# First products two k-tiles at a time behind half jobs of modulation, and the norm parameters and last norm ahead of the loop of rounds

## The chip, the cores and the metric

The kernel runs on one core of a Trainium2 chip. The core has a matrix engine (TensorE; PE for its matmuls, PEld for its weight loads), three engines for elementwise work (VectorE or DVE, ScalarE or ACT, GpSimd or POOL), and SyncE (SP), which issues most of the transfers between the memory of the chip and the core. Each engine works through its own list of instructions in order and waits on semaphores for the others. The metric is the device time of one execution in microseconds (us); lower is better.

## What is computed

Two blocks, each of two layers, on x of 256 tokens by 1024 columns, all in float32.

```python
# block 1, per layer
mod = silu(c) @ w_ada + b_ada                      # 6 * 1024 values: shifts, scales, gains
sh1, sc1, g1, sh2, sc2, g2 = split(mod, 6)
h = rmsnorm(x, norm1_w) * (1 + sc1) + sh1          # "modulation"
u = h @ w_in                                       # pool, conv, q, k, v and gates
x = x + g1 * (merge_of_branches(u) @ w_out)
h2 = rmsnorm(x, norm2_w) * (1 + sc2) + sh2
x = x + g2 * ((silu(h2 @ w_gate) * (h2 @ w_up)) @ w_down)

# block 2
h = layer_norm(x, ln_in_g, ln_in_b)
for l in range(2):
    mix = mixer(h)                                 # three kinds of attention
    h = layer_norm(alpha * h + mix, ln1_g, ln1_b)
    ffn = grouped_moe(h)                           # 16 experts, 2 of one group per token
    h = layer_norm(alpha * h + ffn, ln2_g, ln2_b)  # the last one is the output
```

## The kernel before, in words

**Precision.** A float32 product is built from products of parts: each operand is split into a rounded part and the rest (`split`, a cast on ACT at L278 and a subtraction on DVE at L279 for weights; `hl` holds both parts of the activations), and three matmuls (L321, L322, L323 in `xs_part`) add up one product. The first of the three needs only the cast, the second the subtraction too.

**Order.** PE's list stands in the order in which the code is written. The other engines' lists are put in order by a list scheduler; `tc.issue_after` in the code adds a constraint to it. SP's list holds the weight loads in the order of the code, each into the next unit of a ring of buffers (`use_ring`, `raw`), so a load also waits until its unit is free. A load waits in addition until the load eight places before it has landed.

**The start of the program.** SP issues c, the constants `con`, x, the masks, the bias `b_ada`, the norm rows and the positions, and behind them eight loads of w_ada (`ada_first`) and six of w_in (`first_weights`), 1 MB each. PE turns x (L472), DVE copies the turned x out (L473). `norm_scale` squares the turned x on ACT (L757) and sums over the columns with 16 matmuls by ones (L758). `ada_pe` computes 512 columns of modulation per job: 64 small matmuls (L695, 32 columns of weights by 128 elements), a copy (L682), a transpose (L685), an add of the bias (L686). `modulate` then makes, per k-tile of 128 columns, u on DVE (L769), the rounded part on ACT (L770), the rest on DVE (L771). k-tiles 0 to 3 need jobs 0 and 2 (shift and scale), k-tiles 4 to 7 need jobs 1 and 3. Products run over k-tiles 0 to 3 for q, k and v in turn (j = 0, 1, 2), with jobs 1 and 3 between them, then over k-tiles 4 to 7.

**The mixture of experts** (`moe`). The token's norm is taken, ACT casts the rounded part `hn[0]` (L1500), and POOL (first half, L1502) and DVE (second half, L1569) subtract for the rest `hn[1]`. DVE works out the two experts of each token (L1506 to L1530), PE counts the slots (L1534 to L1538), DVE makes one-hot matrices (L1546), PE gathers 64 slots per expert (L1562). Then eight pairs of experts follow (`pair`): gate products, up products, activation (L1636, L1637), transposes (L1641), copy (L1643), down products, all matmuls at L1597, and the matmuls that put the pair's result back into token order (`combine`, L1656, added to the state at L1658). Those of a pair run inside the next pair; in the last pair they stand between gate and up (`pump(2)`). The statistics of the layer's last norm are taken quarter by quarter in the last pair (L802).

**The loop of rounds.** Behind the pairs each engine reads the number of rounds from memory (L1711), and a hardware loop (L1717) repeats the eight pairs for tokens that found no slot. In the profiled execution its body is not entered; every engine still crosses it with semaphores and branches. Behind the loop, `norm_params` (L810 to L817) turns the statistics into mean and scale. In layer 0 `normalise` (L826, L827) and PE's transposes (L855) then start the next mixer. In layer 1 the gains are spread over the partitions by PE (L833), applied on DVE (L1759, L1760) and, for one quarter, on ACT and POOL (L1750 to L1752), and four output transfers are issued (L1761, L1762).

Of the kernel before, what the change touches and what calls it, by code (L numbers as in the profile page):

```python
# [11 lines left out]
F32 = mybir.dt.float32  # L12
# [8 lines left out]
P = 128  # L21
# [54 lines left out]
def kernel(ctx: ExitStack, tc: tile.TileContext, A, const, out):  # L76
# [92 lines left out]
    RING_START = (17, 18, 19, 20, 21, 15, 16, 3, 4, 8, 10, 17, 18, 19, 20, 21)  # L169
# [4 lines left out]
    RING_MOE = (22, 8, 10, 11, 0, 12, 13, 9, 17, 18, 19, 20, 21, 5, 6, 7, 3, 4)  # L174
    UNIT = {8: 2560}
# [84 lines left out]
    early, held = {}, []  # L260
# [4 lines left out]
    def split(src):  # L265
# [8 lines left out]
        with ExitStack() as es:  # L274
            if held:
                for inst in held.pop():
                    es.enter_context(tc.issue_after(inst.ins))
            S.copy(h, src)  # L278
            V.tensor_sub(lo, src, h)  # L279
# [59 lines left out]
    nc.sync.dma_start(con, const[:, :CONST_KEEP])  # L339
# [22 lines left out]
    nc.sync.dma_start(xn, A["x"].rearrange("o (a p) d -> p (o a) d", p=P))  # L362
    masks = t512()[:, :CONST_W - CONST_KEEP]
    nc.sync.dma_start(masks, const[:, CONST_KEEP:])
    stage = [t512()[:, 0:P], None]
    stage_rows(nc.sync, "b_ada", rows(A["b_ada"]), 48)
    stage_rows(nc.sync, "norm1_w", rows(A["norm1_w"]), 8)
    stage_rows(nc.sync, "norm2_w", rows(A["norm2_w"]), 8)
    posi = cst.tile([P, 2, 2], I32, name="posi")
    nc.sync.dma_start(posi[:, 0, :], A["positions"].rearrange("o (a p) -> p (o a)", p=P))  # L370
    nc.sync.dma_start(posi[:, 1, :], A["positions_2"].rearrange("o (a p) -> p (o a)", p=P))
    use_ring(RING_START)

    def first_weights(k0):

        return [raw(wview(A["w_in"], 0, k0 * P, (k0 + 4) * P, 1024 + 512 * j, 1536 + 512 * j), 4, 512) for j in range(3)]

    ada_first, w_first = {}, []
# [64 lines left out]
    V.tensor_scalar_mul(cs, cact, 0.5)  # L443

# [7 lines left out]
    V.tensor_copy(causalb, mask_of("causal"))  # L452
    chunkb = cst.tile([P, P], BF16, name="chunkb")
    V.tensor_copy(chunkb, mask_of("chunk"))
    beforeb = cst.tile([P, P], BF16, name="beforeb")
    V.tensor_copy(beforeb, mask_of("before"))
# [223 lines left out]
    def ada_out(l, j, ps):  # L680
# [3 lines left out]
        def post():  # L684
            PE.transpose(ps[:, P:T], m, ident)  # L685
# [4 lines left out]
    def ada_pe(l, j, ch):  # L690
        ps = at_bank()
        for k0, r in ch:
            for k in range(k0, k0 + r.shape[1]):
                for q in range(4):
# [1096 lines left out]
```

## Time and profile before

| | |
|---|---|
| time, three runs | 1595.78, 1597.12 (median), 1597.85 us |
| the profiled execution | 1598.5 us, its span 1596.3 us |
| PE busy in the span | 1508.8 us (95%) |
| DVE, ACT, POOL busy | 977.2, 736.9, 251.3 us |
| moved by DMA | 419.71 MB, 263 GB/s over the span |

The profile is one execution, with its times counted from the start of the span. [...] A matmul's length overlaps with its successor's; the distance of starts is the pace.

### The profile page before, as it was taken

What the parts mean: (1) busy time and instruction counts of PE and PEld (TensorE: products, weight loads), DVE (VectorE), ACT (ScalarE), POOL (GpSimd) and SP (SyncE); (2) the same over time, 40 slices, a digit from 0 to 9 for tenths busy, and PEclk for the clock granted to TensorE, in tenths of its full rate; (3) what the DMA queues carried; (4) which work ended last, traced back from release to release, by engine and by line L of the source; (5) the groups of instructions that cost most, each with busy time, mean ns of one, the idle gap of its engine ahead of it and who ended that gap; (6) DMA issues with size and microseconds to landing.
All of it is one profiled execution on the core that took longest, in us unless ns stands there. A gap on an engine that the chain in (4) does not pass through costs nothing. (4 is left out here: it accounts for less than half of the span.)

```text
span 1596.3 us, 24445 instructions
## 1 busy us (share of the span) xinstructions
PE 1508.8 (95%) x9211; PEld 1091.9 (68%) x9211; DVE 977.2 (61%) x1894; ACT 736.9 (46%) x1403; POOL 251.3 (16%) x279
## 2 busy tenths in 40 slices
PE   6999899999999999999998998999998999899996
PEld 5877788888887888888887876344436877344343
DVE  4769777777787767787657667222226776423224
ACT  3466745655446674566546565121115665211122
POOL 0333640001224263100003110000000310000000
PEclk9999999999999999999999998999998999899998
DMA  9666769656864675965535457999995648899995
GB/s 349 240 210 247 253 231 324 204 188 200 314 203 156 211 263 182 321 211 178 173 103 158 150 193 281 366 407 407 407 403 203 217 141 291 310 407 407 407 407 196
DMA packets 278476, 419.71 MB, mean 263 GB/s; under 512 B 12722, under 2 KB 147748, under 8 KB 278348
## 3 DMA queue, kind: packets, MB, share of 16 engines
q1 hardware_dynamic: 273052, 398.63, 70.6%
q0 software_dynamic: 5152, 19.14, 3.5%
q8 instruction: 77, 1.26, 0.3%
q14 instruction: 51, 0.42, 0.1%
q10 hardware_dynamic: 144, 0.26, 0.0%
HBM read 416.94 MB, written 1.05 MB: 262 GB/s over the span
## 5 line engine op out<-in xcount | busy, mean ns | idle before, releaser
L279 DVE TENSOR_TENSOR split<-raw,split 128x1024 fp32r<-128x1024 f32 (+4 forms) x330 | 412.6, 1254 | 113.1 <-ACT split L278 109.9
L289 PE MATMUL mm<-hl,split 128*128 128x512 f32 x1168 | 413.4, 397 | 0.0
L278 ACT CAST split<-raw 128x1024 fp32r<-128x1024 f32 (+4 forms) x330 | 328.8, 1000 | 130.0 <-PE mm L323 68.7
L290 PE MATMUL mm<-hl,split 128*128 128x256 f32 x1168 | 328.0, 281 | 0.6 <-DVE split L279 0.6
L289 PEld LDWEIGHTS mm<-hl,split 128*128 128x128 f32 x1168 | 219.5, 188 | 49.3 <-issue 0.9
L1597 PE MATMUL mm<-raw,xg 128*64 128x512 f32 x1024 | 233.6, 603 | 1.1 <-ACT xg L1564 1.1
L290 PEld LDWEIGHTS mm<-hl,split 128*128 128x128 f32 x1168 | 221.5, 190 | 1.1 <-DVE split L279 0.9
L1597 PEld LDWEIGHTS mm<-raw,xg 128*64 128x64 f32 x1024 | 70.2, 138 | 130.9 <-issue 113.1
L289 PE MATMUL mm<-ahl,split 128*128 128x512 f32 x352 | 123.4, 394 | 0.0
L306 ACT COPY t<-mm 128x256 f32<-128x256 f32 x152 | 56.7, 373 | 143.3 <-PE mm L290 133.4
L1597 PE MATMUL mm<-raw,t 128*64 128x512 f32 (+1 forms) x576 | 114.8, 549 | 1.5 <-ACT t L1643 1.4
L321 PE MATMUL mm<-split,hl 128*128 128x512 f32 (+4 forms) x272 | 102.1, 375 | 4.3 <-ACT split L278 3.2
L290 PE MATMUL mm<-ahl,split 128*128 128x256 f32 x352 | 98.7, 281 | 0.3 <-DVE split L279 0.3
L322 PE MATMUL mm<-split,hl 128*128 128x512 f32 (+4 forms) x272 | 96.0, 353 | 0.9 <-DVE split L279 0.8
L323 PE MATMUL mm<-split,hl 128*128 128x512 f32 (+4 forms) x272 | 96.2, 354 | 0.5 <-POOL hl L1210 0.4
L306 DVE TENSOR_TENSOR t<-mm,t 128x256 f32<-128x256 f32 x140 | 59.2, 423 | 49.5 <-ACT t L306 49.2
L1597 PEld LDWEIGHTS mm<-raw,t 128*64 128x64 f32 x576 | 39.4, 137 | 67.6 <-issue 50.8
L1673 DVE SCALAR_TENSOR_TENSOR t<-mm,s,t 128x512 fp32r<-128x512 f32 (+1 forms) x36 | 24.9, 691 | 91.8 <-ACT t L1672 91.8
L289 PEld LDWEIGHTS mm<-ahl,split 128*128 128x128 f32 x352 | 65.9, 187 | 15.0 <-ACT t L1095 0.2
L1672 ACT ACTIVATE t<-mm,s 128x512 fp32r<-128x512 f32 (+1 forms) x36 | 23.1, 640 | 106.0 <-PE mm L1597 106.0
L1643 ACT COPY t<-at 128x512 f32<-128x512 f32 x16 | 9.4, 588 | 129.9 <-PE at L1641 129.9
L290 PEld LDWEIGHTS mm<-ahl,split 128*128 128x128 f32 x352 | 66.5, 189 | 0.6 <-DVE split L279 0.6
(426 smaller groups left out, 2504.8 us busy)
## 6 DMA issues: line engine op xcount, KB each, us to landing
raw<-in_exp_w_gate_dram SPq DMA_DIRECT2D x128, 512.0 KB
raw<-in_exp_w_up_dram SPq DMA_DIRECT2D x128, 512.0 KB
raw<-in_exp_w_down_dram SPq DMA_DIRECT2D x128, 512.0 KB
raw<-in_w_in_dram SPq DMA_DIRECT2D x54, 1024.0 KB
raw<-in_w_ada_dram SPq DMA_DIRECT2D x30, 1024.0 KB
raw<-in_w_gate_dram SPq DMA_DIRECT2D x22, 1024.0 KB
raw<-in_w_up_dram SPq DMA_DIRECT2D x22, 1024.0 KB
ada<-in_w_ada_dram POOLq DMA_DIRECT2D x18, 1024.0 KB, 6.6
```

What stands on the lines that cost most here:

```text
L278: S.copy(h, src)
L279: V.tensor_sub(lo, src, h)
L289: PE.matmul(ps, h[:, k], x[k0 + k], start=first and k == 0, stop=False)
L290: PE.matmul(ps[:, :T], lo[:, k], x[k0 + k][:, :T], start=False, stop=last and k == K - 1)
L306: return S.copy(b[:, :T], ps[:, T:]), V.tensor_add(dst, ps[:, :T], b[:, :T])
L321: PE.matmul(ps[i][:, :n], xh, h[:, j], start=f, stop=False)
L322: PE.matmul(ps[i][:, :n], xh, lo[:, j], start=False, stop=False)
L323: PE.matmul(ps[i][:, :n], xl, h[:, j], start=False, stop=z)
L1597: PE.matmul(ps[64 * b:64 * b + 64, :], lhs(k, b), ws[k][b], start=k == 0, stop=k == nk - 1)
L1643: S.copy(aT, pb)
L1672: S.activation(yh[:, sl], pd_[:, :w], AF.Copy, scale=gs)
L1673: V.scalar_tensor_tensor(yl[:, sl], pd_[:, :w], gs, yh[:, sl], op0=OP.mult, op1=OP.subtract)
```

## The change

**Start.** Constants, masks, bias, norm rows and positions are loaded from ACT's queue. x comes in two halves. Jobs 0 and 2 of the modulation are split into half jobs of 256 columns (`ada_first[j, h]`), and w_in's first loads hold two k-tiles each, 1 MB for q and k together and 0.5 MB for v. `first_scale` squares x as it was loaded, with its tokens on the partitions, sums on ACT, and spreads the result with two matmuls; the 16 matmuls by ones go. Products now run over k-tiles 0 and 1, then 2 and 3, then 4 to 7, with half jobs and jobs 1 and 3 between the first six. `rotary_tables` is put behind the second modulation. The casts of three masks move from DVE to POOL.

**Routing.** The subtraction of the first half of `hn[1]` moves from POOL to DVE, behind the slot positions.

**Last pair.** The matmuls of the pair before are no longer put between gate and up; they come behind up, around the transposes. The loads of the next layer (layer 0) or two of the spread gains (layer 1) are put ahead of the last pair's down products.

**Loop.** The number of rounds is read in the middle pair. `norm_params` and, in layer 1, the whole last norm with its four output transfers stand ahead of the loop, and again at the end of its body. In layer 0 `normalise` follows the loop in smaller pieces, with the first split of the next weights behind it.

```diff
-    nc.sync.dma_start(xn, A["x"].rearrange("o (a p) d -> p (o a) d", p=P))
+    for a in range(2):
+        nc.sync.dma_start(xn[:, a], A["x"][0, a * P:(a + 1) * P])
...
-        return [raw(wview(A["w_in"], 0, k0 * P, (k0 + 4) * P, 1024 + 512 * j, 1536 + 512 * j), 4, 512) for j in range(3)]
+        qk_, v_ = [raw(wview(A["w_in"], 0, k0 * P, (k0 + 2) * P, a, b), 2, b - a) for a, b in ((1024, 2048), (2048, 2560))]
+        w_first[k0] = [qk_[:, :, 0:512], qk_[:, :, 512:1024], v_]
     for h_ in range(2):
-        for j in (h_, 2 + h_):
-            ada_first[j] = k_chunks(A["w_ada"], 0, KD, 512 * j, 512 * j + 512)
-        if h_ == 0:
-            w_first.append(first_weights(0))
+        for j in (0, 2):
+            ada_first[j, h_] = k_chunks(A["w_ada"], 0, KD, 512 * j + 256 * h_, 512 * j + 256 * h_ + 256)
+        first_weights(2 * h_)
+    for j in (1, 3):
+        ada_first[j] = k_chunks(A["w_ada"], 0, KD, 512 * j, 512 * j + 512)
...
+    def first_scale():
+        ss, y, h, z, rs = small(2), small(2), small(2), small(2), small(2)
+        sq = unit(13, "sq").rearrange("p (a d) -> p a d", a=2)
+        for i in range(2):
+            S.activation(sq[:, i], xn[:, i], AF.Square, accum_out=ss[:, i:i + 1])
...
+            PE.matmul(pb[:, i * P:(i + 1) * P], rs[:, i:i + 1].to_broadcast([P, P]), ident, start=True, stop=True)
...
-            ada_pe(0, 0, ada_first[0])
-            ada_pe(0, 2, ada_first[2])
+            for j in (0, 2):
+                ada_pe(0, j, ada_first[j, 0], 0)
             pump()
-            w_first.append(first_weights(4))
-            modulate(hl, 0, 0, "norm1_w", acc, range(4))
+            first_weights(4)
+            modulate(hl, 0, 0, "norm1_w", acc, range(2))
+            for k0 in (0, 2):
+                for j in range(3):
...
+                    xs_part(pss[j], [(k0, w_first[k0][j])], hl, 512, KD, 1)
+                    if j < 2 and k0 == 0:
+                        ada_pe(0, 2 * j, ada_first[2 * j, 1], 1)
+                    elif j < 2:
+                        ada_pe(0, 1 + 2 * j, ada_first[1 + 2 * j])
+                if k0 == 0:
+                    first_weights(6)
+                    modulate(hl, 0, 0, "norm1_w", acc, range(2, 4))
+            last = modulate(hl, 0, 0, "norm1_w", acc, range(4, 8))
+            with tc.issue_after(last.ins):
+                rotary_tables()
...
-                    if q == 0:
-                        G.tensor_sub(hn[1][:, i, sl], y[:, i, sl], hn[0][:, i, sl])
...
-        for i in range(2):
-            last = V.tensor_sub(hn[1][:, i, 512:], y[:, i, 512:], hn[0][:, i, 512:])
+        with tc.issue_after(placed.ins):
+            for sl in (slice(0, 256), slice(256, 512), slice(512, 1024)):
+                for i in range(2):
+                    last = V.tensor_sub(hn[1][:, i, sl], y[:, i, sl], hn[0][:, i, sl])
...
-            if done:
-                pump(2)
             proj(pu, xs, wu, KD)
...
+                if p == NPAIR // 2:
+                    loads, (rounds,) = nc.values_load_multi_w_load_instructions(nri[0:1, 0:1], min_val=1, max_val=4)
...
-        rounds = nc.values_load(nri[0:1, 0:1], min_val=1, max_val=4)
-        if l + 1 < L:
-            mixer_first(l + 1)
+        keep = sml.tile([P, 8], F32, tag="keep", name=nm("keep"), bufs=1)
+        norm_params(keep)
+        if l + 1 == L:
+            last_norm(keep, lnb)
...
         with tc.For_i(1, rounds, 1):
...
+            norm_params(keep)
+            if l + 1 == L:
+                last_norm(keep, lnb)
         if l + 1 < L:
             use_ring(first_ring)
             mixer_ahead(l + 1)
+            held.append(normalise(keep[:, 4:6], keep[:, 6:8]))
+            split_early(wf[0][1][:, 0:2])
+            held.append(last_split[0])
```

`last_norm` is new; its work is that of the deleted end of the kernel, into a buffer `res` of its own:

```python
def last_norm(keep, gb):
    g_, b_ = [[gain_bank(f"ln2_{L - 1}", v, q, mm_bank()) for q in range(2)] for v in range(2)]
    mean, rs, nb = keep[:, 0:4:2], keep[:, 4:6], keep[:, 6:8]
    r, t = res[0], st[0]
    rq = r[:, 1, 0:512]
    S.activation(rq, t[:, 1, 0:512], AF.Identity, bias=nb[:, 1:2], scale=rs[:, 1:2])
    G.tensor_mul(rq, rq, gb[0])
    G.tensor_add(rq, rq, gb[1])
    ...
            V.scalar_tensor_tensor(r[:, i, sl], t[:, i, sl], mean[:, i:i + 1], g_[q], op0=OP.subtract, op1=OP.mult)
            V.scalar_tensor_tensor(r[:, i, sl], r[:, i, sl], rs[:, i:i + 1], b_[q], op0=OP.mult, op1=OP.add)
            nc.sync.dma_start(out[0, i * P:(i + 1) * P, sl], r[:, i, sl])
    nc.scalar.dma_start(out[0, P:T, 0:512], rq)
```

How the lists move, at three places. First DVE's list of the kernel before from the end of modulation job 3 on: `scw` is the scale, `t` the u of a k-tile, `split_519` the first weights of k-tiles 4 to 7.

```order
L682 COPY t_466<-at_433 128x128
L686 TENSOR_TENSOR mod<-at_433,cols 128x4
L279 TENSOR_TENSOR split_519<-raw_309,split_519 128x1024
L765 SCALAR_TENSOR_TENSOR scw<-mod,cols 128x4
L769 SCALAR_TENSOR_TENSOR t_503<-xT_140,scw,t_222 128x256
...
L769 SCALAR_TENSOR_TENSOR t_515<-xT_140,scw,t_222 128x256
L771 SCALAR_TENSOR_TENSOR hl_234<-t_503,mod,hl_234 128x256
```

The same place of DVE's list in the changed kernel, where `split_527` is the first split of k-tiles 4 to 7.

```order
L688 COPY t_473<-at_440 128x128
L698 TENSOR_TENSOR mod<-at_440,cols 128x4
L798 SCALAR_TENSOR_TENSOR scw<-mod,cols 128x4
L802 SCALAR_TENSOR_TENSOR t_493<-xT_145,scw,t_202 128x256
...
L802 SCALAR_TENSOR_TENSOR t_505<-xT_145,scw,t_202 128x256
L804 SCALAR_TENSOR_TENSOR hl_211<-t_493,mod,hl_211 128x256
...
L804 SCALAR_TENSOR_TENSOR hl_211<-t_505,mod,hl_211 128x256
L627 CAST s_509<-posi 128x4
L279 TENSOR_TENSOR split_527<-raw_254,split_527 128x1024
```

The split moved from ahead of the second modulation to behind it: ten more instructions stand between the end of job 3 and the subtraction for which the second matmul of k-tile 4 waits.

Next DVE's list of the kernel before in the routing of layer 0, from the masks of the chosen experts to the gates: `oh` are one-hot matrices, `hn` the rest of the normed state.

```order
L1530 SCALAR_TENSOR_TENSOR mb_10170<-s_10158,s_10155 128x32
L1530 SCALAR_TENSOR_TENSOR mask_10171<-s_10158,s_10155 128x32
L1541 SCALAR_TENSOR_TENSOR pos_10184<-at_10178,mask_10171 128x32
L1546 TENSOR_TENSOR oh_10186<-pos_10184,con 128x256 x2
L1546 TENSOR_TENSOR oh_10519<-pos_10184,con 128x256 x2
L1569 TENSOR_TENSOR hn_10112<-state_8374,hn_10111 128x512 x2
L1575 TENSOR_TENSOR gate_10204<-s_10129,mask_10171 128x32
```

The same stretch of DVE's list in the changed kernel.

```order
L1611 SCALAR_TENSOR_TENSOR mb_10176<-s_10164,s_10161 128x32
L1611 SCALAR_TENSOR_TENSOR mask_10177<-s_10164,s_10161 128x32
L1622 SCALAR_TENSOR_TENSOR pos_10190<-at_10184,mask_10177 128x32
L1653 TENSOR_TENSOR hn_10120<-state_8382,hn_10119 128x256
L1627 TENSOR_TENSOR oh_10192<-pos_10190,con 128x256 x2
L1653 TENSOR_TENSOR hn_10120<-state_8382,hn_10119 128x256 x3
L1653 TENSOR_TENSOR hn_10120<-state_8382,hn_10119 128x512 x2
L1659 TENSOR_TENSOR gate_10214<-s_10137,mask_10177 128x32
```

Four subtractions of 256 columns came in, one of them ahead of the first one-hot matrices, and two one-hot matrices of the next group went to a later place.

Last the end of SP's list in the kernel before: the last weight loads, which belong to the loop's body, the loop's branches and the output.

```order
L1684 DMA raw_16983<-in_exp_w_down_dram 128x2x512 x2
L1684 DMA raw_16986<-in_exp_w_down_dram 128x2x512 x2
L1684 DMA raw_16989<-in_exp_w_down_dram 128x2x512 x2
L1717 REGISTER_ALU
L1717 COMPARE_AND_BRANCH
L1717 UNCONDITIONAL_BRANCH
L1761 DMA out_dram<-state_8374 128x512 x3
L1787 UNCONDITIONAL_BRANCH
```

The end of SP's list in the changed kernel.

```order
L1771 DMA raw_17048<-in_exp_w_down_dram 128x2x512 x2
L1771 DMA raw_17051<-in_exp_w_down_dram 128x2x512 x2
L1771 DMA raw_17054<-in_exp_w_down_dram 128x2x512 x2
L1555 DMA out_dram<-res_15856 128x512 x3
L1825 REGISTER_ALU
L1825 COMPARE_AND_BRANCH
L1825 UNCONDITIONAL_BRANCH
```

No output transfer is left behind the loop; the three in the body are the repetition, and three like them stand ahead of the loop. The branch that leaves the loop waits in both kernels for the semaphores of all transfers that are under way.

## Rows read from the trace of the kernel before

**Rows 1.** Windows: start and end, length, PE, PEld, DVE, ACT, POOL busy, granted clock, DMA share, GB/s.
```profile
0.00:27.55 27.55, 12.95 (x165) 11.09 (x165) 11.95 (x49) 10.05 (x20) 3.16 (x10) 0.97 0.93 322
27.55:67.77 40.22, 39.76 (x274) 32.00 (x275) 26.60 (x49) 18.07 (x23) 3.92 (x3) 0.93 0.88 321
1100.00:1195.00 95.00, 94.94 (x454) 38.05 (x454) 24.00 (x46) 15.68 (x28) 0.00 (x0) 1.00 1.05 406
1582.80:1596.30 13.50, 2.07 (x4) 1.15 (x4) 5.43 (x14) 3.46 (x5) 2.54 (x2) 0.50 0.21 80
```

**Rows 2.** Timeline of the start: start, length, engine, line, operation, [idle before, releaser].
```profile
10.23 3.67 PE L472 MATMUL at<-con,xn 128*128 128x128 f32 x16 [5.95 <-DMA xn<-in_x_dram]
24.34 0.16 DVE L686 TENSOR_TENSOR mod<-at,cols 128x4 f32<-128x4 f32 x1 [0.32 <-PE at L685]
27.55 0.80 PE L321 MATMUL mm<-split,hl 128*128 128x512 f32 x1 [3.24 <-ACT split L278]
```

**Rows 3.** Timeline around the second modulation.
```profile
43.87 1.95 PE L695 MATMUL at<-raw,cs 128*32 128x128 f32 x64
47.64 1.23 DVE L279 TENSOR_TENSOR split<-raw,split 128x1024 fp32r<-128x1024 f32 x1
48.97 1.67 DVE L769 SCALAR_TENSOR_TENSOR t<-xT,scw,t 128x256 f32<-128x256 f32 x4
50.56 1.67 DVE L771 SCALAR_TENSOR_TENSOR hl<-t,mod,hl 128x256 fp32r<-128x256 f32 x4
51.45 0.39 PE L321 MATMUL mm<-split,hl 128*128 128x512 f32 x1
```

**Rows 4.** Timeline of PE: a later hole, and a matmul behind it.
```profile
133.85 0.70 PE L1021 MATMUL at<-vn,up 128*128 128x256 f32 x2 [2.41 <-DVE vn L1017]
136.12 0.63 PE L289 MATMUL mm<-hl,split 128*128 128x512 f32 x1
```

**Rows 5.** Timeline of the routing of layer 0.
```profile
986.88 2.50 POOL L1502 TENSOR_TENSOR hn<-state,hn 128x512 fp32r<-128x512 f32 x2 [46.28 <-ACT hn L1500]
987.25 0.92 DVE L1524 TENSOR_TENSOR s<-s,s 128x8 f32<-128x8 f32 x1
988.20 1.22 DVE L1530 SCALAR_TENSOR_TENSOR mb<-s,s 128x32 bf16<-128x32 f32 x1
989.34 0.18 DVE L1530 SCALAR_TENSOR_TENSOR mask<-s,s 128x32 f32<-128x32 f32 x1
989.47 0.19 PE L1534 MATMUL at<-mb,beforeb 128*128 128x16 bf16 x1 [4.48 <-DVE mb L1530]
991.39 1.29 DVE L1569 TENSOR_TENSOR hn<-state,hn 128x512 fp32r<-128x512 f32 x2
```

**Rows 6.** Waits of SP's queue from 990 to 1040: total, times, longest.
```profile
SPq L1684 <- PE mm L1597: 25.7, 10, 12.0
```

**Rows 7.** Timeline of PE in the last pair of layer 1.
```profile
1558.84 2.13 PE L1656 MATMUL at<-t,got 128*128 128x512 f32 x8
1568.78 0.66 PE L1641 MATMUL at<-con,t 128*128 128x128 f32 x4 [0.79 <-DVE t L1637]
1570.16 2.16 PE L1597 MATMUL mm<-raw,t 128*64 128x256 f32 x18 [0.72 <-ACT t L1643]
```

**Rows 8.** Timeline behind the loop of layer 0.
```profile
1213.05 0.39 DVE L810 BATCH_NORM_AGGREGATE s<-s 128x2 f32<-128x24 f32 x2 [2.21 <-issue]
1215.44 3.67 PE L855 MATMUL at<-con,state 128*128 128x128 f32 x16 [5.82 <-ACT state L826]
1218.79 0.69 PE L321 MATMUL mm<-split,hl 128*128 128x384 f32 x1
```

**Rows 9.** The loop's branches on PE: count, shortest, median, longest ns, first and last start.
```profile
L1717 PEldq COMPARE_BRANCH  x6: 82/190/3593, 1209.7 to 1586.6; - x6
```

**Rows 10.** Timeline behind the loop of layer 1.
```profile
1584.69 0.39 DVE L810 BATCH_NORM_AGGREGATE s<-s 128x2 f32<-128x24 f32 x2 [2.02 <-issue]
1591.74 0.75 DVE L1760 SCALAR_TENSOR_TENSOR state<-state,s,at 128x512 f32<-128x512 f32 x1
```

More of the change, by code (lines that the diff above doesn't have):

```diff
@@ L684, in post @@
         def post():
+            if h is not None:
+                o = 4 * j + 2 * h
+                PE.matmul(ps[:, P:P + 2], m, adasel, start=True, stop=True)
+                V.tensor_add(mod[:, l, o:o + 2], ps[:, P:P + 2], colr(f"b_ada{l}", o, o + 2))
+                return
             PE.transpose(ps[:, P:T], m, ident)
@@ L822, in normalise @@
         t = st[0]
+        if src is None:
+            for q in range(2):
+                sl = slice(256 * q, 256 * q + 256)
+                for i in range(2):
+                    last = S.activation(t[:, i, sl], t[:, i, sl], AF.Identity, bias=nb[:, i:i + 1], scale=rs[:, i:i + 1])
+            for i in range(2):
+                last_v = V.tensor_scalar(t[:, i, 512:], t[:, i, 512:], rs[:, i:i + 1], nb[:, i:i + 1], op0=OP.mult, op1=OP.add)
+            return last, last_v
         for q in range(2):
@@ L1618, in combine_T, with pair @@
             yield got, gs[:, 0:1]
-        def pair(p, xg, more, oh, wg, wu, wd, done=None):
+        def pair(p, xg, more, oh, wg, wu, wd, done=None, ahead_of_down=None):
             def xs(k, b):
@@ L1642, in pair @@
             aT = t512()
-            S.copy(aT, pb)
+            turned_a = S.copy(aT, pb)
+            order = ahead_of_down(turned_a) if ahead_of_down else ()
             if done:
@@ L1701, in experts, with next_weights @@
             return wg, wu, wd
+        lnb, wf = [], []
+        def next_weights(behind_):
+            if l + 1 < L:
+                wf[:] = mixer_first(l + 1)
+                return ()
+            for v in range(2):
+                lnb.append(unit(U_LAST[v], "lnb")[:, :512])
+            with tc.issue_after(behind_.ins):
+                return [(S.copy(lnb[v], gain_bank(f"ln2_{l}", v, 0)),) for v in range(2)]
         for p in range(NPAIR):
@@ L1708, in moe @@
                     next(more)
-            pair(p, xg, more, oh, *experts(p, p == NPAIR - 1), done=stats if p == NPAIR - 1 else None)
-        rounds = nc.values_load(nri[0:1, 0:1], min_val=1, max_val=4)
-        if l + 1 < L:
-            mixer_first(l + 1)
-        loop_ring = tuple(u for u in RING_MOE if l + 1 == L or u not in ring["units"])
+            end = p == NPAIR - 1
+            with ExitStack() as es:
+                if p == NPAIR // 2:
+                    loads, (rounds,) = nc.values_load_multi_w_load_instructions(nri[0:1, 0:1], min_val=1, max_val=4)
+                    for inst in loads:
+                        es.enter_context(tc.issue_after(inst.ins))
+                pair(p, xg, more, oh, *experts(p, end), done=stats if end else None, ahead_of_down=next_weights if end else None)
+        keep = sml.tile([P, 8], F32, tag="keep", name=nm("keep"), bufs=1)
+        norm_params(keep)
+        if l + 1 == L:
+            last_norm(keep, lnb)
+        taken = ring["units"] if l + 1 < L else U_LAST
+        loop_ring = tuple(u for u in RING_MOE if u not in taken)
         first_ring = ring["units"]
```

140 lines of the change are left out of this document (73 added, 67 removed).

## The prediction

> **What bounds the kernel now.** I read the windows first. In the middle of a stretch of experts PE is busy 94.94 of 95.00 us at a granted clock of 1.00 [rows 1]; there nothing that the change touches can gain, except by letting the stretch begin earlier or by shortening what follows it. The places with idle PE are four, and the change edits each: the start (12.95 us of work in 27.55), the routing of each layer (PE waits 4.48 us for DVE's `mb` [rows 5]), the activation of the last pair (0.79 and 0.72 us [rows 7]), and the stretch behind the loop of rounds (PE 2.07 us of 13.50 [rows 1]). Then I read the timeline at each place for the wait that ends last.
>
> **Start.** Before, the first product starts at 27.55. What leads up to it: x lands, the first turn runs at 10.23 for 3.67 us, then come the 16 matmuls by ones and the modulation jobs 0 and 2, whose last add is at 24.34; from there it is 3.21 us to the product, through `scw`, u and the cast of the weights [rows 2]. After, 16 matmuls and half of both jobs go. x starts 0.7 us sooner, an estimate, since only c stands ahead of it in SP's list, and PE is through with the turn and two small matmuls at about 14.4. The two half jobs need 1 MB behind x; at the 322 GB/s of this window [rows 1] that is 3.1 us, so they are there by then. A full job of 64 matmuls takes 1.95 [rows 3], so two halves take about 2.0, copy, turn and add another 1.0: the add falls at 17.4, the product at 17.4 + 3.21 = 20.6. That is 7.0 us sooner. Bounds: 19.0 if x lands 1.6 sooner, 23.5 if the half jobs land 3 us later.
>
> [...] With x at 10.23 as before, the sum would be 0.7 us worse; no row of this case shows loads from ACT's queue at the start.
>
> How much of the 7.0 us reaches the end of the phase at 67.77? The clock is the first loss. The hole of 3.24 us ahead of 27.55 left PE below its full level: the phase shows 0.93 over 40.22 us [rows 1], which is 2.8 us. A hole of the same kind (17.4 to 20.6) stays, so this loss stays. From 20.6 then: 72 products of k-tiles 0 to 3 at a pace of 0.227 (72 of them fill 51.45 to 67.77 [rows 1, 3]), 16.3; the second half jobs and jobs 1 and 3, 2.0 + 3.9; the clock, 2.8; and a new stall ahead of k-tiles 2 and 3, where mod, u, remainder and split follow the half jobs on DVE beside only 12 products. Its price is not shown; it lies between 0 and 3.2 (the whole way from add to product), and I take 1.5. Job 3 then ends before the last 12 products, at 20.6 + 16.3 + 5.9 + 2.8 + 1.5 - 2.7 = 44.4, against 45.82 before.
>
> The second loss is the order on DVE. Before, the split for k-tile 4 starts at 47.64, 1.82 after job 3's end, ahead of `scw`, and u and the remainder are hidden behind the products that run until 51.45 [rows 3]. After, that subtraction stands behind `scw`, four u (1.67), four remainders (1.67) and a cast of positions. The second matmul of k-tile 4 needs it: 44.4 + 1.82 + 0.2 + 1.67 + 1.67 + 0.2 + 1.23 = 51.2. PE is done with k-tile 3 at 47.1, so it is idle for nearly 4 us but for one matmul. Behind the waiting matmul stand all 71 others and everything of PE: 51.2 + 16.1 = 67.3. Elsewhere a hole of 2.41 us was followed by matmuls of 0.63 where 0.39 is the full level's [rows 3, 4]; so I charge the clock once more, with 2.1, three quarters of 2.8. The phase ends at about 69.4, **+1.6 us**. Bounds: -4.8 (neither clock loss, 2.8 and 2.1, nor the stall is paid: 69.4 - 6.4 = 63.0), +4 (first product at 23.5, the stall full, less of the last hole).
>
> The rotary tables now lie on DVE behind the second modulation; they hide in the 16 us of products that follow. The mask casts on POOL are needed hundreds of microseconds later, and cost nothing; if POOL is late, it costs the 0.2 us of a cast.
>
> **Routing.** While POOL subtracts for 2.50 us, DVE's two operations beside it take 0.92 and 1.22; the one of the same shape as the latter, right behind it, takes 0.18 [rows 5]. They end last before PE's 4.48 us wait. With POOL out of it `mb` is 1.04 sooner and L1524 some 0.7. DVE gets four subtractions of 256 columns, 0.32 each by half of 0.65 (1.29 for two of 512 [rows 5]); one stands ahead of the one-hot matrices, the others before the half that DVE already made and beside PE's gather. -1.04 - 0.7 + 0.32 = -1.4, in two layers **-2.8**. It reaches the end of the layer since SP waits 25.7 us there for PE to free units [rows 6]: the weight stream moves with PE. Bounds -4.0 and 0.
>
> **Last pair.** The eight matmuls of the pair before (2.13 us) now lie in the two holes (0.79 + 0.72) in place of standing ahead of up [rows 7]. Layer 0: -1.5. In layer 1 two gain matmuls come along, 0.26 each at the full level (four take 2.07 at the 0.50 of that window [rows 1]): -1.0. Together **-2.5**, bounds -3.0 and 0. Reading the number of rounds amid the pairs puts a load into every list; PE has matmuls queued, I charge **+0.3** (0 to 1).
>
> **Behind layer 0.** The statistics end 2.21 us before 1213.05, at D = 1210.84; turning starts at D + 4.60 and the first product at D + 7.95 [rows 8]. PE comes out of its branch after up to 3.59 us [rows 9]. After, mean and scale (1.5 us) stand ahead of the branch, so PE arrives 1.5 later and turns at about D + 5.2; normalise is done by then and the split ready, so the product follows after 1.7 in place of 3.35: D + 6.9, **-1.0** (-2 to +1).
>
> **Behind layer 1.** D is 1582.67, the last DVE work ends at 1592.49, the span at 1596.3 [rows 1, 10]: landing and final barrier take 3.8. After, six operations of 0.7 on DVE, the parameters and POOL's two operations of 1.27 start at D; the last output is issued at D + 7.0 where it was D + 9.9. But SP's branch waits for the landing, and then PE takes its 3.59: D + 7.0 + 3.8 + 3.6 = D + 14.4 against D + 13.6, **+0.8**. Bounds: -2 if the branch of 3.59 lies beside the landing, +1.5.
>
> [...]
>
> **Sum.** 1.6 - 2.8 - 2.5 + 0.3 - 1.0 + 0.8 = -3.6. The profiled execution took 1598.5, 2.2 around its span and 1.4 above the median, so I put the sum on the median: 1597.1 - 3.6 = **1593.5 us**.
>
> **Rivals.**
> (a) *The start keeps its gain.* If products stay at the full level through both holes and the half jobs' modulation is early enough, the phase ends at -4.8 in place of +1.6: total -3.6 - 6.4 = -10.0, or 1587.1. For it: 7 us are cut off ahead of the first product. Against it: ten instructions stand before the split, and the trace shows the clock lost after holes no longer than these.
> (b) *The weight stream sets the end of the experts.* It moves 406 GB/s while PE is busy [rows 1], so little is left to spare; if units rather than PE time the stream, the 2.8 of the routing and half of the last pair are waited off later. Total +1.6 - 1.2 + 0.3 - 1.0 + 0.8 = +0.5: 1597.6. Against it: PE waits for 0.06 us in that window.
> (c) *The clock stays low from the first product to k-tile 4.* Three holes (3.2, 1.5, 4 us) now follow one another with about 10 us of work between. At the half level the pace of 72 products is 0.45 instead of 0.23; if all of k-tiles 0 to 3 ran so, the phase would lose 16.3 - 2.8 = 13.5 more, of which the hole at k-tile 4 does not shrink: +1.6 + 9 to 13. It makes the kernel slower once it takes more than 3.6 us off the forecast, which is 16 products more at the half level. With half of the 72 so, total -3.6 + 8.1 = +4.5: 1601.6. Against it: before, the low level ended about 5 us after work began, as 0.93 over 40.22 says (2.8 lost is 5.6 us at the half level).
> (d) *Gains and losses are each smaller*, every term at half: 1595.3; it belongs to the forecast.
>
> **Chances.** Forecast with (d) 0.47, (a) 0.20, (b) 0.18, (c) 0.15. The forecast's own range is 1590 to 1597. What a measurement can tell from no change is 0.2%, 3.2 us. Faster by more: half of the forecast, nearly all of (a), 0.46 together with a rest of (b). Within it: the other half, most of (b), some of (c), 0.37. Slower: (c) and the bad end of (b), 0.17. The range is 1587 to 1601: it reaches to (a) and nearly to (c).
>
> **What would show it.** First product (L322) near 21 to 22, PE idle for some 4 us before the second matmul of k-tile 4 and a granted clock below 1 behind it, the first matmul of L289 at about 69. In the routing `mb` takes 0.2, and PE's wait before it is shorter by 1.0 to 1.7. In the last pair of both layers PE has no hole between up and down. Behind layer 0 the first product comes 6.9 after the last statistics. At the end an output transfer lands before PE's long branch, and the span ends some 14.4 after D. The forecast is wrong if the first matmul of L289 comes before 66 or after 73, if PE's branch runs beside the landing, or if the expert stretch begins earlier and does not end earlier.

## The result: slower by 1.3%, where 0.2% faster was forecast

The changed kernel takes 1620.55 us (median of 4 runs, 1616.60 to 1622.17), the kernel before 1597.38 (1595.78 to 1597.85). The ratio is 1.0128, with a 95% interval of 1.0109 to 1.0148. The forecast of 1593.5 and its whole range, 1587 to 1601, are missed. The time went to a place that none of my steps looked at: the buffers for the weights start 32 bytes later than before, and the stream of loads into them is 5% slower.

### The profile page after: what moved, and what is told of

Read it like the earlier page. It is cut to its first block, busy times and chain, and to the rows that moved or that the text cites. A ratio compares the mean times of both kernels' runs of the same rounds, so it can differ in the third digit from the quotient of the medians.

```text
span 1618.9 us, 24449 instructions
## 1 busy us (share of the span) xinstructions
PE 1526.2 (94%) x9207; PEld 1094.6 (68%) x9207; DVE 975.9 (60%) x1906; ACT 733.7 (45%) x1400; POOL 247.2 (15%) x278
## 3 DMA queue, kind: packets, MB, share of 16 engines
HBM read 416.94 MB, written 1.05 MB: 258 GB/s over the span
## 5 line engine op out<-in xcount | busy, mean ns | idle before, releaser
L289 PE MATMUL mm<-hl,split 128*128 128x512 f32 x1168 | 413.4, 397 | 1.6 <-DVE qkn L946 1.6
L289 PEld LDWEIGHTS mm<-hl,split 128*128 128x128 f32 x1168 | 219.5, 188 | 51.1 <-ACT t L306 1.8
L1681 PE MATMUL mm<-raw,xg 128*64 128x512 f32 x1024 | 246.6, 606 | 5.0 <-DMA raw<-in_exp_w_up_dram 2.3
L289 PE MATMUL mm<-ahl,split 128*128 128x512 f32 x352 | 123.4, 395 | 0.0
L289 PEld LDWEIGHTS mm<-ahl,split 128*128 128x128 f32 x352 | 65.9, 187 | 15.2 <-ACT t L1145 0.2
L1719 DVE SCALAR_TENSOR_TENSOR t<-t,mm 128x512 f32<-128x512 f32 x16 | 11.0, 688 | 97.8 <-PE mm L1681 97.8
```

What stands on the lines that cost most here:

```text
L289: PE.matmul(ps, h[:, k], x[k0 + k], start=first and k == 0, stop=False)
L1681: PE.matmul(ps[64 * b:64 * b + 64, :], lhs(k, b), ws[k][b], start=k == 0, stop=k == nk - 1)
L1719: V.scalar_tensor_tensor(a, th, 0.5, pu, op0=OP.mult, op1=OP.mult)
```

## The profile after

The first lines of the page of the changed kernel:

```profile
span 1618.9 us, 24449 instructions
...
PE 1526.2 (94%) x9207; PEld 1094.6 (68%) x9207; DVE 975.9 (60%) x1906; ACT 733.7 (45%) x1400; POOL 247.2 (15%) x278
```

PE shows 17 us more busy time with nearly the same number of matmuls (9207, and 9211 before), and the other engines no more work than before. So it is not added work. The windows that answer to [rows 1], of the changed kernel (from the start to its first product, from there to the first matmul of L289, the stretch of experts, and from the last statistics to the end):

```profile
0.00:20.68 20.68, 7.89 (x91) 6.40 (x91) 8.08 (x33) 7.31 (x13) 3.94 (x13) 0.97 0.94 293
20.68:70.39 49.71, 45.69 (x342) 34.96 (x343) 30.46 (x66) 19.66 (x27) 3.49 (x2) 0.91 0.84 296
1100.00:1195.00 95.00, 94.33 (x443) 38.26 (x440) 22.35 (x42) 17.16 (x30) 0.00 (x0) 1.00 1.05 386
1604.00:1618.90 14.90, 0.00 (x0) 0.00 (x0) 4.92 (x14) 1.11 (x2) 2.53 (x2) 0.58 0.20 75
```

The third line is the one to look at. The transfer engines are as full as before (share 1.05), but move 386 GB/s in place of 406, and PE gets through 443 matmuls in place of 454 at the same granted clock of 1.00. SP's queue shows the same group by group. Of the changed kernel, groups of loads of 512 KB in a row:

```profile
1110.74 10.01 SPq L1771 DMA_DIRECT2D raw<-in_exp_w_gate_dram  x8
1121.57 10.19 SPq L1771 DMA_DIRECT2D raw<-in_exp_w_up_dram  x8
1132.50 10.13 SPq L1771 DMA_DIRECT2D raw<-in_exp_w_down_dram  x8
```

Of the kernel before, groups of the same kind:

```profile
1110.82 9.87 SPq L1684 DMA_DIRECT2D raw<-in_exp_w_up_dram  x8
1121.11 9.87 SPq L1684 DMA_DIRECT2D raw<-in_exp_w_down_dram  x8
1131.39 9.87 SPq L1684 DMA_DIRECT2D raw<-in_exp_w_gate_dram  x8
```

From one start to the next it is 10.28 us for eight loads before and 10.83 to 10.93 after. A layer has 24 such groups, so its stream is up to 14 us longer. PE was 94.94 of 95.00 us busy before because the stream, with what was loaded ahead, was just quick enough; now PE waits for it. PE's waits in the stretch of layer 0 (in all, times, longest), and two stretches of its last pair, of the changed kernel:

```profile
PE mm L1681 <- DMA raw<-in_exp_w_up_dram: 1.2, 4, 0.3
PE mm L1681 <- DMA raw<-in_exp_w_gate_dram: 0.8, 3, 0.3
...
1198.83 2.43 PE L1681 MATMUL mm<-raw,xg 128*64 128x512 f32 x8 [0.27 <-DMA raw<-in_exp_w_up_dram]
1201.55 2.42 PE L1681 MATMUL mm<-raw,xg 128*64 128x512 f32 x8 [0.29 <-DMA raw<-in_exp_w_up_dram]
```

The waits come late. Until about 1165 PE keeps its old pace (321 matmuls from 1100 to 1165, and as many in the kernel before from 1094 to 1159), on weights that were loaded ahead, though the loads are slower from the first group that nothing else holds up (10.85 us from 1034.92 on). In the last pair eight matmuls then take 2.72 us from start to start, the time of two loads, where they took 1.74 before; 0.3 of that is listed as a wait, and the rest is counted as longer matmuls, so it stands in PE's larger busy time. The size is read from marks: from the first gate product to the last combining matmuls it was 992.71 to 1208.48 in layer 0, 215.8 us; now it is 998.11 to 1222.30, 224.2 us. Layer 1 gives 9 us more in the same way. That is 17.6 of the 22.6 us by which the span grew. The shorter last pair hides a part of it: in the changed kernel with its buffers back in place (below) the two stretches take 213.8 and 214.4 us, so the slower stream cost 20.9 of the 23.0 us between the two.

In the program the units (the buffers that weights land in, among others) are one pool, laid out behind the pool of constants. The change adds one constant, `adasel`, of 8 bytes per partition; it takes 32, and the first unit starts at byte 14368 of each partition where it started at 14336. The latter is a multiple of 256, the former is not.

## The experiments

All ratios are to the kernel before on the same chip; one hundredth is 16 us.

**One pad of 32 bytes in the kernel before.**

```diff
+    pad = cst.tile([P, 2], F32, name="pad")
+    V.memset(pad, 0.0)
     cs = cst.tile([P, KD], F32, name="cs")
```

> The kernel before with one more tile of 8 bytes per partition (a pad, filled once, never read) ahead of the units, which moves every unit by 32 bytes. Theory address (the small tile adasel moved all buffers by 32 bytes, and writes into buffers that start there land 5% slower): the expert stretch moves 386 in place of 407 GB/s, a group of eight 512 KB loads takes 10.86 in place of 10.28 us, and the time is 1597 + 18 to 22 = about 1617. Theory queue (the constants on ACT's queue or the loads with 1 KB rows make the later weight stream slower): no change, 1597, 407 GB/s. Theory order (the new order of the instructions costs it): no change, 1597.

Measured: 1619.99 us, ratio 1.0141 (1.0119 to 1.0162). Its stretch of experts:

```profile
1100.00:1195.00 95.00, 94.06 (x435) 38.49 (x434) 22.47 (x43) 16.89 (x30) 0.00 (x0) 1.00 1.05 386
```

None of the change is in this kernel but the shift of the buffers, and it is as slow as the changed one. The theories of ACT's queue and of the order have fallen.

**One pad of 64 bytes.** The same edit with 16 elements in place of 2.

> The kernel before with a pad of 64 bytes per partition ahead of the units. Theory address says nothing yet of which boundary counts: if units on a multiple of 64 bytes are enough, 407 GB/s and 1597; if they must start on a larger power of two, about 386 GB/s and 1617. Theories queue and order: 1597.

Measured: 1619.89 us, ratio 1.0135 (1.0115 to 1.0155).

```profile
1100.00:1195.00 95.00, 93.95 (x428) 37.83 (x428) 22.36 (x44) 15.69 (x28) 0.00 (x0) 1.00 1.05 386
```

A start on a multiple of 64 was not enough, and 64 bytes off cost what 32 cost: 386 GB/s in both.

**The changed kernel with its units back in place.**

```diff
-    adasel = cst.tile([P, 2], F32, name="adasel")
+    adasel = sml.tile([P, 2], F32, tag="adasel", name="adasel", bufs=1)
```

> The changed kernel with adasel taken from the pool behind the units, so that the units start where they did before; nothing else is changed. Theory address: 407 GB/s in the expert stretches, and the time falls by 18 to 23 to about 1598 to 1602 (the sum of my steps, as the trace of after sizes them, is +2.6 start, -1.8 routing of layer 0, -1.8 routing of layer 1, -0.6 behind layer 0, +1.3 end, the last pairs -1 to -2.5: -1 to -3, so 1594 to 1597 if the weight stream is all that is wrong). Theory queue: 386 GB/s stays, 1620. Theory order: 407 GB/s may come back, but the time stays above 1610.

Measured: 1597.85 us, ratio 0.9991 (0.9979 to 1.0003).

```profile
1100.00:1195.00 95.00, 94.94 (x462) 38.40 (x460) 22.29 (x42) 17.05 (x30) 0.00 (x0) 1.00 1.05 406
```

Eight bytes put elsewhere give back all that was lost, 0.0137 of the ratio or 22 us. What is left of the change is -1.4 us, with an interval that reaches +0.5: no change that could be told. My sum of its parts was -3.6.

**Where the boundary is: 128 bytes off.**

```diff
-    rwb = cst.tile([P, L, N_EXP], F32, name="rwb")
+    rwb = sml.tile([P, L, N_EXP], F32, tag="rwb", name="rwb", bufs=1)
```

> The kernel before with one table of 128 bytes per partition (rwb) taken from the pool behind the units, so that every unit starts 128 bytes earlier, on a multiple of 128 but not of 256 bytes. If a multiple of 128 is enough for the landing writes: 407 GB/s in the expert stretch, 10.28 us for eight loads of 512 KB, about 1598. If it must be 256 or more: 386 GB/s, 10.86 us, about 1618.

Measured: 1621.64 us in one run, where the kernel before takes 1600.30 on the same chip.

```profile
1100.00:1195.00 95.00, 93.94 (x437) 37.94 (x434) 21.63 (x41) 16.40 (x29) 0.00 (x0) 1.00 1.05 386
```

**And 256 bytes off.**

```diff
-    identb = cst.tile([P, P], BF16, name="identb")
+    identb = sml.tile([P, P], BF16, tag="identb", name="identb", bufs=1)
```

> The kernel before with one table of 256 bytes per partition (identb) taken from the pool behind the units, so that every unit starts 256 bytes earlier, on a multiple of 256 but not of 512 bytes. If 256 is the boundary: 407 GB/s and about 1598. If 512 or more: 386 GB/s and about 1618. If both this and the shift by 128 bytes run at 386, the boundary is larger than 256, or only the old place is good.

Measured: 1598.13 us in one run on that chip.

```profile
1100.00:1195.00 95.00, 94.93 (x453) 37.72 (x452) 23.54 (x43) 15.05 (x27) 0.00 (x0) 1.00 1.05 406
```

So, of the starts that were tried, 256 bytes is the boundary for these loads, whose rows are 2 KB: starts off by 32, 64 and 128 bytes all move 386 GB/s, starts off by 0 and 256 move 406. Each of the shifts moves every unit, also those that engines compute in; that the loads themselves are slower is read from their packets (last section).

**The early split.** With the units in place, the split for k-tile 4 is asked for ahead of the second modulation.

```diff
+            split_early(w_first[4][0][:, 0:2])
             last = modulate(hl, 0, 0, "norm1_w", acc, range(4, 8))
```

> The changed kernel with adasel behind the units, and besides the first split of the weights of k-tile 4 asked for ahead of the second modulation: on DVE it then stands behind three u instead of behind four u, four remainders and a cast. If the order on DVE makes the hole of 2.9 us at k-tile 4 and the half clock behind it, the hole shrinks to about 1 us, the clock stays at 1.00, and the first matmul of L289 comes 3 to 4 us sooner than in the changed kernel with aligned units; the time falls by the same 3 to 4. If instead POOL's or DVE's work behind the phase sets the next step, the phase ends sooner and the time falls by less than 1.

Measured: 1595.50 us, ratio 0.9981 (0.9967 to 0.9994). The holes of PE at k-tile 4, of this kernel:

```profile
49.74 0.50 PE L322 MATMUL mm<-split,hl 128*128 128x512 f32 x1 [0.88 <-DVE split L279]
...
54.74 0.50 PE L322 MATMUL mm<-split,hl 128*128 128x512 f32 x1 [1.43 <-DVE split L279]
```

The hole shrank from 2.93 to 0.88, as expected, and the granted clock stays at 1.00 behind it (50 to 60, where it is 0.83 in the changed kernel). But a second hole of 1.43 opens at the next split. From the first product to the first matmul of L289 it is 48.3 us (19.92 to 68.25) in place of 49.8 (21.86 to 71.67): 1.5 where 3 to 4 were expected; the first matmul of L289 comes 3.4 sooner, but 1.9 of that stands ahead of the first product, which the edit does not touch. In time the gain is 0.0010 of the ratio, less than the intervals can tell.

**The old start.** All of the change but its start, units in place.

```diff
-    for a in range(2):
-        nc.sync.dma_start(xn[:, a], A["x"][0, a * P:(a + 1) * P])
+    nc.sync.dma_start(xn, A["x"].rearrange("o (a p) d -> p (o a) d", p=P))
...
-            for j in (0, 2):
-                ada_pe(0, j, ada_first[j, 0], 0)
+            ada_pe(0, 0, ada_first[0])
+            ada_pe(0, 2, ada_first[2])
```

> The changed kernel with the whole start undone (small loads on SP's queue, 512-column jobs, four k-tiles at a time, squares of the turned x), everything behind block 1's start as changed; units start where they did before. By the traces the changed start ends its phase 2.6 to 3.9 us later than the old one: the first matmul of L289 goes back to 67.8 and the time falls by 2.5 to 4 against the changed kernel with aligned units, to about 1594. If the start pays nothing (what is lost there is made up in the attention that follows), the time stays at 1598.

Measured: 1594.12 us, ratio 0.9959 (0.9947 to 0.9972); the first matmul of L289 is at 67.68. The new start costs 0.0032 or 5 us by the ratio, the old one is better. The phase itself accounts for 1.7 to 4.0 of it: in the three kernels with the new start, no early split and units in place, the first matmul of L289 is at 69.39, 70.19 and 71.67.

**Output transfers behind the loop.** The early split's kernel, with the last norm ahead of the loop as changed, and its transfers behind.

```diff
-                nc.sync.dma_start(out[0, i * P:(i + 1) * P, sl], r[:, i, sl])
-        nc.scalar.dma_start(out[0, P:T, 0:512], rq)
...
+        if l + 1 == L:
+            for q, i in ((0, 0), (1, 0), (1, 1)):
+                sl = slice(512 * q, 512 * q + 512)
+                nc.sync.dma_start(out[0, i * P:(i + 1) * P, sl], res[0][:, i, sl])
+            nc.scalar.dma_start(out[0, P:T, 0:512], res[0][:, 1, 0:512])
```

> The changed kernel with aligned units and the early split, and the four output transfers issued behind the loop of rounds in place of ahead of it (the last norm stays ahead). If the landing of the output stands in series with PE's branch of 3.6 us, as my term for the end had it, the branch now runs beside the landing: from the end of the last statistics to the end of the span 11 us in place of 14.9, and 3 to 4 us less than with the early split alone, about 1592. If the branch costs its 3.6 us wherever it stands, or the final barrier waits for something else, 14 to 15 us stay and the time does not change.

Measured: 1592.32 us, ratio 0.9950 (0.9938 to 0.9963), 0.0031 or 5 us below the early split's, where 3 to 4 were expected. Its end (the last statistics, the output, and PE's branch between 1582.9 and 1588: count, shortest, median, longest ns, first and last start):

```profile
1582.50 0.74 DVE L836 BATCH_NORM_STATS2 s<-state 128x6 f32<-128x256 f32 x2
...
1590.15 1.61 SPq L1842 DMA_DIRECT2D out_dram<-res  x3
```

```profile
L1824 PEldq COMPARE_BRANCH  x1: 3647/3647/3647, 1583.3 to 1583.3; - x1
```

The output is issued 6.9 us after the statistics (1583.24), and the span ends 12.3 us after them, against 14.8 in the changed kernel and 14.6 with the early split alone. So the move saves 2.3 to 2.5 us between these marks, but what it takes out is not PE's branch, as my term had it: PE's long branch starts at 1583.3, right behind the statistics, and is over at 1587.0, before the output is issued. What went is a pause of SP. In the changed kernel SP passes a branch behind the landing, and its next instruction comes 2.6 us later (its rows stand with the end, below). Here SP passes that branch at 1576.4, amid the last pair, pauses 2.7 us there, and then waits until 1588.9 anyway. From the last landing to the end of the span it is 1.5 us (1594.1 to 1595.6) where it was 5.3 (1613.5 to 1618.9); 1.4 of that is given back, since the output is issued later. The expected 11 was not reached: I had counted from the first transfer, and SP issues its third at 1591.04.

**Both.** The old start with the transfers behind the loop.

> The changed kernel with the whole start undone and the output transfers behind the loop. If the two gains stand apart (start about 3.5 us, end about 2 to 3 us against the changed kernel with aligned units), the ratio to before is 0.993 to 0.994, about 1589 where before is 1599. If they share a cover, it is no better than either alone, 0.995 to 0.996.

Measured: 1592.44 us, ratio 0.9954 (0.9939 to 0.9970); its profiled span, 1588.7, is the shortest of all kernels here, but the runs do not tell it from the output behind the loop with the new start and early split, or from the old start alone. The two gains did not add up by the ratio (0.993 to 0.994 was expected if they did), which I leave open: the intervals of 0.003 are as wide as the gain that is missing.

**The old routing**, units in place.

```diff
+                    if q == 0:
+                        G.tensor_sub(hn[1][:, i, sl], y[:, i, sl], hn[0][:, i, sl])
...
-        with tc.issue_after(placed.ins):
-            for sl in (slice(0, 256), slice(256, 512), slice(512, 1024)):
-                for i in range(2):
-                    last = V.tensor_sub(hn[1][:, i, sl], y[:, i, sl], hn[0][:, i, sl])
+        for i in range(2):
+            last = V.tensor_sub(hn[1][:, i, 512:], y[:, i, 512:], hn[0][:, i, 512:])
```

> The changed kernel with aligned units and the old routing (POOL subtracts the first half of the rest of the normed state). If my term for the routing holds, PE's wait ahead of the slot counts goes back from 2.7 to 4.5 us and the gather starts 1.4 to 1.8 us later in each layer counted from the router's last product; the time rises by about 3 against the changed kernel with aligned units. If the shift is waited off again by the weight stream, the wait grows but the end of the experts stays.

Measured: 1602.04 us, ratio 1.0015 (1.0004 to 1.0026). PE's wait is back, and POOL's subtraction with it:

```profile
989.55 2.49 POOL L1585 TENSOR_TENSOR hn<-state,hn 128x512 fp32r<-128x512 f32 x2 [46.27 <-ACT hn L1583]
...
990.87 1.22 DVE L1613 SCALAR_TENSOR_TENSOR mb<-s,s 128x32 bf16<-128x32 f32 x1
...
992.14 0.20 PE L1617 MATMUL at<-mb,beforeb 128*128 128x16 bf16 x1 [4.48 <-DVE mb L1613]
```

Against the aligned kernel the ratio rises by 0.0024 or 3.8 us, where 3 were expected: the gain of the routing is real and carries to the end.

**The old last pair**, units in place.

```diff
             got, gs = box
+            if done:
+                pump(2)
             proj(pu, xs, wu, KD)
```

> The changed kernel with aligned units and the matmuls of pair 6 put back between gate and up of the last pair; the loads and gains ahead of down stay. By my term the holes of 0.79 and 0.72 us come back ahead of the transposes and ahead of down in both layers (less what the two gain matmuls fill in layer 1), and the time rises by 2.5. If the holes close otherwise, it stays.

Measured: 1601.01 us, ratio 1.0009 (0.9999 to 1.0020), 0.0018 or 2.9 us above the aligned kernel; the two intervals just overlap. PE in the last pair of layer 0, where both holes are back:

```profile
1196.59 0.66 PE L1725 MATMUL at<-con,t 128*128 128x128 f32 x4 [0.79 <-DVE t L1721]
1197.96 3.24 PE L1681 MATMUL mm<-raw,t 128*64 128x256 f32 x28 [0.72 <-ACT t L1727]
```

## Why the prediction was wrong, point by point

**The step that failed** is none of the sum's terms, but what they rest on: the stretch of experts was taken over with its 406 GB/s ("there nothing that the change touches can gain"), and the shift of its begin was carried through since "the weight stream moves with PE". The part-by-part list has every instruction and transfer of the change, but not its memory: `adasel` does not appear in it. A tile of 8 bytes ahead of the weight buffers made the stream 5% slower, 386 GB/s in place of 406, and the stream had no 5% to give. Eight loads took 10.28 us, 30.8 for the three groups of a pair, while PE needs 23.8 and 28.6 us for a pair in turn (the down products of four pairs in a row started at 1039.08, 1067.70, 1091.47 and 1120.07), 26.2 on average. So already before PE lived on what was loaded ahead, and it lasted to the end of the layer; at 32.5 us for a pair it ran out in the last one. The row behind "moves with PE", SP's 25.7 us of waits for PE [rows 6], is of 990 to 1040 alone; from 1059 to 1183 a group of eight loads started every 10.28 us, by the pace of the loads. Rival (b), the weight stream as the bound, named the right resource with a chance of 0.18; but it was priced at the old rate, +0.5, and its point against, that PE never waits, was true only of that rate.

**Start, forecast +1.6.** The first product was put at 20.6 and is at 20.68. The rows that answer to [rows 2, 3], of the changed kernel's timeline:

```profile
13.88 0.68 PE L789 MATMUL at<-con,s 128*128 128x128 f32 x4 [1.60 <-DVE s L786]
...
20.68 0.80 PE L321 MATMUL mm<-split,hl 128*128 128x512 f32 x1 [2.84 <-ACT split L279]
...
26.58 1.08 PE L710 MATMUL at<-raw,cs 128*32 128x128 f32 x32
...
30.78 1.08 PE L710 MATMUL at<-raw,cs 128*32 128x128 f32 x32
...
43.94 1.95 PE L710 MATMUL at<-raw,cs 128*32 128x128 f32 x64
...
48.03 1.67 DVE L802 SCALAR_TENSOR_TENSOR t<-xT,scw,t 128x256 f32<-128x256 f32 x4
49.62 1.67 DVE L804 SCALAR_TENSOR_TENSOR hl<-t,mod,hl 128x256 fp32r<-128x256 f32 x4
...
51.27 1.22 DVE L279 TENSOR_TENSOR split<-raw,split 128x1024 fp32r<-128x1024 f32 x1
...
52.55 0.50 PE L322 MATMUL mm<-split,hl 128*128 128x512 f32 x1 [2.92 <-DVE split L279]
...
54.54 0.63 PE L322 MATMUL mm<-split,hl 128*128 128x512 f32 x1
...
70.39 0.39 PE L289 MATMUL mm<-hl,split 128*128 128x512 f32 x1
```

That the first product fits to 0.1 us is in part luck: the second half of x was turned from 8.61 on, 1.6 us sooner than before and not 0.7, and PE then waited 1.6 us for the scale that `first_scale` makes, a wait that the sum did not have. In the other three kernels with this start and no early split the first product is at 19.72, 20.35 and 21.86. At k-tile 4 every link is there: the split behind four u, four remainders and the cast, the hole, a granted clock of 0.50 behind it (54 to 56, where a matmul takes 0.63), the end of the phase at 70.39, +2.6. Sizes: the stall ahead of k-tiles 2 and 3, charged with 1.5, is 0.5 (PE waits 0.49 for the split at 36.06). Job 3 still ends at 45.9, not 44.4, since a group of 12 products between two jobs takes 3.2 us and not 2.7 (26.58 to 30.78 less the job's 1.0); the pace of 0.227 is that of a long run. The hole is 2.9 and not nearly 4. In the three kernels with units in place the phase ends at 69.39, 70.19 and 71.67, +1.6 to +3.9; from first product to end it is 49.7 to 49.8 us in all four, so the spread is that of the first product. Rival (a) fell, since DVE's order did bind; rival (c) fell too: the granted clock, 0.50 over 25 to 26, was 0.95 over 26 to 27 and 1.00 from 30 to 40.

**Routing, forecast -1.4 per layer.** The answer to [rows 5], of the changed kernel:

```profile
994.42 0.19 DVE L1611 SCALAR_TENSOR_TENSOR mb<-s,s 128x32 bf16<-128x32 f32 x1
...
994.67 0.19 PE L1615 MATMUL at<-mb,beforeb 128*128 128x16 bf16 x1 [2.68 <-DVE mb L1611]
...
996.12 2.29 DVE L1653 TENSOR_TENSOR hn<-state,hn 128x256 fp32r<-128x256 f32 x5
```

`mb` takes 0.19 as forecast, and PE waits 1.8 us less; from the router's first product to the gather it is 9.2 us (986.8 to 996.0) in place of 10.8 (979.8 to 990.6), so -1.6. Right in place and size, and shown by the run that undoes it.

**Last pair, forecast -2.5.** The answer to [rows 7], of the changed kernel, layer 1:

```profile
1588.02 1.20 PE L1739 MATMUL at<-t,got 128*128 128x512 f32 x4
1589.05 0.60 PE L1723 MATMUL at<-con,t 128*128 128x128 f32 x4
1589.58 0.73 PE L875 MATMUL at<-lnrow,lnsel 64*128 64x512 f32 x2
1590.37 1.20 PE L1739 MATMUL at<-t,got 128*128 128x512 f32 x4
1591.50 3.24 PE L1681 MATMUL mm<-raw,t 128*64 128x256 f32 x28
```

PE has no hole between up and down, as forecast. In the aligned kernel, where no load is waited for, up's end and down's start lie 2.5 us apart in layer 0 (1195.47 to 1197.98) and 3.5 in layer 1 (1565.30 to 1568.79); before it was the two holes and the transposes, 2.2, and eight matmuls ahead of up, 2.1 by the same pace: -1.8 and -0.8. Right, and undoing it costs 2.9 us by the ratio, where the two intervals just overlap. The +0.3 for reading the number of rounds is not seen: the products around the read keep their pace (7.0 us from the down products at 1097.48 to the gather at 1104.50, and as much before).

**Behind layer 0, forecast -1.0.** The statistics end at 1224.66 and the first product is 7.35 us later, where 7.95 was before and 6.9 was forecast (7.2 to 7.7 in the kernels with units in place); the answer to [rows 8], of the changed kernel:

```profile
1223.91 0.75 DVE L836 BATCH_NORM_STATS2 s<-state 128x6 f32<-128x256 f32 x2
...
1228.68 3.68 PE L897 MATMUL at<-con,state 128*128 128x128 f32 x16 [5.25 <-DVE state L863]
...
1232.01 0.67 PE L321 MATMUL mm<-split,hl 128*128 128x384 f32 x1
```

PE turns 4.0 us after the statistics, sooner than the 5.2 forecast: its long branch does not wait for mean and scale but starts at 1223.63, ahead of the statistics' end, so the 1.5 us that the sum charged for them were not paid. The product then follows 3.3 later, as before, and not 1.7: PE's own 16 turns fill that time without a hole, at a granted clock of 0.50 (1228.68 to 1232.00), and not the split. The sign was right, the size -0.2 to -0.7, by two wrong steps that nearly cancel.

**The end, forecast +0.8.** From the statistics to the end of the span it is 14.8 us (1604.02 to 1618.86), where 14.4 was forecast and 13.6 was before; 14.4 to 14.8 in the kernels with this end and units in place. The answer to [rows 10], of the changed kernel, and the branches of PE and SP in 1604 to 1608, in 1613.8 to 1616, and SP's next semaphores:

```profile
1607.77 2.46 SPq L1555 DMA_DIRECT2D out_dram<-res  x3
...
1610.66 0.38 ACTq L1556 DMA_DIRECT2D out_dram<-res  x1
```

```profile
L1825 PEldq COMPARE_BRANCH  x1: 3318/3318/3318, 1604.1 to 1604.1; - x1
...
L1825 SPq COMPARE_BRANCH  x1: 33/33/33, 1614.0 to 1614.0; - x1
L1825 PEldq COMPARE_BRANCH  x1: 179/179/179, 1614.5 to 1614.5; - x1
...
L1825 SPq EVENT_SEMAPHORE  x12: 28/28/28, 1616.6 to 1617.3; - x12
```

The size is right, the step is not. The sum had PE's 3.6 us behind the landing. PE's long branch starts at 1604.1, right behind the statistics, and is over at 1607.4, before the first output is issued at 1607.77; the branch that PE takes behind the landing, at 1614.5, lasts 0.18. What does stand behind the landing is SP: it passes its branch at 1614.0, its next instruction starts at 1616.6, and the other engines wait for SP at the end of the program until 1617.8. So 2.6 us of SP stood in for 3.6 of PE, and the forecast came near by luck. [Rows 9] could not tell: the row gives the longest of six branches and the start of the last, and in the kernel before too these are two branches, the long one at 1581.64 and the last at 1586.63. In the changed kernel PE's other four branches take 0.08 to 0.19 us.

**The sum of the parts.** Start +1.6 to +3.9, routing -3.2, last pair -2.6, behind layer 0 -0.7 to -0.2, end +0.8 to +1.2: -4.1 to -0.9, against -3.6 forecast and -1.4 measured with the units in place. The interval of the latter, -3.4 to +0.5, holds most of that; the forecast's -3.6 lies just outside it. The range of the prediction was missed by what the sum did not contain.

## What to carry to other kernels

Count a change's memory as well as its instructions: whatever is allocated ahead of the buffers that transfers land in moves them all (here by 32 bytes, with 386 GB/s in place of 406), so keep such a pool at a fixed start, a multiple of 256 bytes in this case, or put new small tiles behind it, and compare the buffers' start bytes of the two programs before anything else. Where a stretch is fed just in time, read its rate in GB/s next to PE's busy share: here PE was busy 94.94 of 95.00 us, and its stream had no slack at all. Here the wait for transfers ahead of the loop's exit held back all that SP still had to do there, 2.6 us behind the landing; with the transfers issued behind the loop SP had its pause of 2.7 us at 1576.4, ahead of the output at 1590.15. And a row that gives the longest of several branches does not say which of them it is: look for its start before charging it to a place.

## What the runs showed of the hardware that was not expected

Loads of weights with rows of 2 KB into buffers that start off a multiple of 256 bytes moved 386 GB/s in place of 406, for 32, 64 and 128 bytes off alike. Eight loads of 512 KB took, from the start of one group to the next, 10.28 us before and 10.29 when 256 off, and 10.84, 10.85 and 10.85 when 32, 64 and 128 off. In the trace the packets of 2 KB took 84.1 ns on average before and 88.1 in the changed kernel, 32 off (1100 to 1195); in the start (20 to 65) it is 84.3 and 87.8. Why it is one price is not settled by these runs.

Around a loop that is not entered, one of PE's three branches took 3.3 to 3.6 us in each layer of the kernels before and after, PE's others 0.2 or less, and those of the other engines 0.06 or less. Behind its second branch SP's next instruction came 2.4 to 2.6 us later, in each layer of both; what fills that time no row shows.
